# Joined h2 products in raw buffers, and GpSimd casts for the first feed-forward block

## The chip, the core and the metric

The kernel runs on one core of one Trainium2 chip. The metric is device time in microseconds of one execution. The core's engines are named in the profile as PE (TensorE, matrix products; PEld its weight loads), DVE (VectorE), ACT (ScalarE), POOL (GpSimd) and SP (SyncE, which issues the DMAs). Each engine works through its own list of instructions; between engines they wait for each other by semaphores.

## The reference

One decoder layer for 256 prompt tokens and 8 x 4 sample tokens (288 tokens in all). Cut to what the change touches:

```python
mod = (silu(c) @ w_ada + b_ada).reshape(n, N_MOD, 1, D_MODEL)
sh_m, sc_m, gt_m, sh_f, sc_f, gt_f = [mod[:, i] for i in range(N_MOD)]
...
x = x + gt_m * (merged @ w_out)
h2 = _rms(x, g_ffn) * (1 + sc_f) + sh_f
gate, up = jnp.split(h2 @ w_ffn_in, 2, axis=-1)
x = x + gt_f * ((silu(gate) * up) @ w_ffn_out)
...
y = _rms(x, g_final)
```

D_MODEL is 2048, D_FF 5632. `h2` is the second modulation; the "root" is the reciprocal root of the mean square of `x`, one factor for each token.

## The kernel before

Activations lie with features on the 128 partitions and the 288 tokens along a row: `x` is 16 tiles of 128 x 288. Weights stream from memory in blocks of 128 x 2048 (1 MB) into a ring of five raw buffers (`RAW = 5`). Products are made at nearly fp32 precision from two parts each: `hi` is the operand rounded to fp32r, `lo` is what the rounding left. A product of a weight tile with an activation tile is three matmuls: hi with hi, hi with lo, lo with hi.

A weight block is split in four segments of 512 columns. `Blk.high` (line 452) casts a segment to `hi` on ScalarE, `Blk.low` (line 464) subtracts on VectorE to get `lo`. There are four `hi` and four `lo` buffers (`SPB = 4`), so a segment can be cast only when TensorE has done its products with the segment four before it.

The stretch in question is the start of the feed-forward part:

- Four blocks `fk` (class `KBlk`) make the first four output tiles of the first feed-forward product from gained but not yet normalised tiles of `x` (`xg`), since the root of the new `x` is not known yet. Each has four segments, and each segment serves one tile of `xg` with 12 matmuls of 128 x 298.
- While they run, `rstd2` and `norm2` make the root and spread it over the partitions (`rb2`), and `mk_h2` makes the 16 tiles of `h2` in three portions: tiles 0 to 5 ahead of the second fk block in the program, 6 to 10 ahead of the third, 11 to 15 ahead of the fourth.
- Then the blocks `fi` follow, the rest of the first feed-forward product, each one output tile over all 16 tiles of `h2` (48 matmuls of 128 x 288). The first of them needs all 16 tiles of `h2` in turn.

A tile of `h2` passes through `modulate` (line 303): VectorE multiplies the tile of `x` with the root (`normed`, into a slot buffer); ScalarE applies gain and shift to the 256 prompt columns (`affine`) and GpSimd does so for the 32 sample columns in two operations (lines 311 and 312); ScalarE casts the result to `hi`; VectorE subtracts for `lo`. The tiles of this chain come from a pool `t` of five buffers.

Up to this stretch the order on ScalarE, VectorE and SyncE is pinned by hand; from the step after the wE blocks on (line 1062) a scheduler orders each engine's instructions by readiness and place in the program. Most instructions of VectorE, ScalarE and SyncE go through one helper and bear line 115 in the profile.

Of the kernel before, what the change touches and what calls it, by code (L numbers as in the profile page):

```python
# [7 lines left out]
F32 = mybir.dt.float32  # L8
F32R = mybir.dt.float32r
ALU = mybir.AluOpType  # L10
AF = mybir.ActivationFunctionType

P = 128
D = 2048
T = 288
# [7 lines left out]
RAW = 5  # L23
# [43 lines left out]
def decoder_kernel(tc, d):  # L67
    nc = tc.nc
    with ExitStack() as es:
        def pool(name, bufs=1, **kw):  # L70
            return es.enter_context(tc.tile_pool(name=name, bufs=bufs, **kw))

        pc = pool("const")
        pw = pool("wstream")
        pslot = pool("slots", SLOTS)
        ptmp = pool("tmp", 5)
        pps = pool("psum", 4, space=bass.MemoryType.PSUM)
        _body(tc, nc, d, pc, pw, pslot, ptmp, pps)


def _body(tc, nc, d, pc, pw, pslot, ptmp, pps):
    ids = [0]

    def nm(s):
        ids[0] += 1
        return f"{s}_{ids[0]}"

    def const(name, shape, dt=F32):
        return pc.tile(shape, dt, tag=name, name=name)

    def slot(dt=F32, shape=(P, T)):
        return pslot.tile(list(shape), dt, tag="s", name=nm("s"), padded_shape=[P, TU])

    def tmp(n=T):
        return ptmp.tile([P, n], F32, tag="t", name=nm("t"), padded_shape=[P, TU])
# [10 lines left out]
    class Pinned:  # L106
        def __init__(self, eng):
            self.eng, self.on, self.last = eng, True, None
# [13 lines left out]
    V, A, G, PE, SY = Pinned(nc.vector), Pinned(nc.scalar), nc.gpsimd, nc.tensor, Pinned(nc.sync)  # L122
# [16 lines left out]
    x = const("x", [P, 16, T])  # L139
# [27 lines left out]
    gm2 = const("gm2", [P, 16, NC])  # L167
# [58 lines left out]
    def sam(ap):  # L226
        return ap.rearrange("p (b s) -> p b s", s=NS)

    def bc4(ap):
        return ap.unsqueeze(2).to_broadcast([P, NB, NS])  # L230
# [10 lines left out]
    def upper(a, n=T):  # L241
        hi = slot(F32R, (P, n))
        A.copy(halves(hi, n), parity(a, n))
        return hi

    def lower(a, hi, n=T):
        lo = slot(F32R, (P, n))
        V.tensor_tensor(halves(lo, n), parity(a, n), halves(hi.bitcast(F32), n), ALU.subtract)
        return lo
# [5 lines left out]
    def normed(kt, rb):  # L255
        t = slot()
        V.tensor_tensor(t, x[:, kt, :], rb, ALU.mult)
        return t
# [10 lines left out]
    def warm(n, after=None):  # L269
        ps = psmisc()  # L270
        with behind(after):
            for _ in range(n):
                PE.matmul(ps[:, :P], ones, ones, start=True, stop=True)
# [9 lines left out]
    class Modulate:  # L283
# [13 lines left out]
        def high(self):  # L297
            self.hi = upper(self.h)
# [4 lines left out]
    def modulate(ks, get, gm, sh0, out):  # L303
        hs, his = {}, {}

        def affine(k, t):
            h = tmp()
            A.activation(
                h[:, :TP], t[:, :TP], AF.Identity, bias=mod[:, sh0 + k, 0:1], scale=gm[:, k, 0:1]
            )  # L310
            G.tensor_tensor(sam(h[:, TP:]), sam(t[:, TP:]), bc4(gm[:, k, 1:]), ALU.mult)  # L311
            S["aff"] = G.tensor_tensor(sam(h[:, TP:]), sam(h[:, TP:]), bc4(mod[:, sh0 + k, 1:]), ALU.add)
            hs[k], his[k] = h, upper(h)

        def finish_(k):
            out[k] = (his[k], lower(hs[k], his[k]))

        ts = {}
        n = len(ks)
        for i in range(n + 2):  # L320
            if i < n:
                ts[i] = get(ks[i])
            if 1 <= i <= n:
                affine(ks[i - 1], ts.pop(i - 1))
            if i >= 2:
                finish_(ks[i - 2])
# [16 lines left out]
    class Step:  # L343
        defer = False
        after, lead = None, 0
        raw = None
# [79 lines left out]
    class Blk(Step):  # L426
        def __init__(self, name, idx, rhs, sink, n=T):
            self.name, self.idx, self.rhs, self.sink, self.n = name, idx, rhs, sink, n
            self.k0, self.nk, self.nm = STREAMS[name]
            n = self.nk * self.nm  # L430
            self.per = -(-n // -(-n // SEG))
            self.segs = [(s, min(n, s + self.per)) for s in range(0, n, self.per)]
            self.his, self.parts, self.then = [], [], {}
            self.cuts = self.mate = self.wide = None
            self.apart = False

        def load(self, at=0, n=None):
# [12 lines left out]
            SY.dma_start(self.raw[:, a:b], d[self.name][self.idx][:, a:b])  # L450

        def high(self):
            s, e = self.segs[len(self.his)]
            hi = pw.tile([P, (e - s) * 128], F32R, tag="hi", name=nm("hi"), bufs=SPB, padded_shape=[P, SEG * 128])
            for a, b, raw in self.spans(s, e):
                self.cast = A.copy(hi[:, a:b], raw)
            self.his.append(hi)

        def spans(self, s, e):
# [90 lines left out]
    def ada(name):  # L550
        u = units[name]
        return [Ada(u, b) for b in range(16 // u[3])]


    S = {"strict": True}
# [274 lines left out]
    h2, xg = {}, {}  # L830
# [11 lines left out]

    def mk_h2(k0, k1):
        def f():
            modulate(range(k0, k1), lambda k: normed(k, S["rb2"]), gm2, 48, h2)

        return Do(f)

# [3 lines left out]
    def sink_fi(i, ps):  # L852
        f, up = i // 2, i % 2
        if not up:
            S["gate"] = ps
            return
        pg = S.pop("gate")
        t = tmp()
        A.activation(t, pg[:, :T], AF.Tanh, scale=0.5)
        V.scalar_tensor_tensor(t, t, 1.0, pg[:, :T], ALU.add, ALU.mult)  # L860
        V.scalar_tensor_tensor(t, t, 0.5, ps[:, :T], ALU.mult, ALU.mult)
        act[f] = split(t)
# [125 lines left out]
    def weave(main, side, a, b):  # L988
        out, n = [], len(side)
        done = 0  # L990
        for i, s in enumerate(main):
            out.append(s)
            want = n if i >= b else max(0, (i - a + 1) * n // (b - a + 1))
            for v in side[done:want]:
                out += v
            done = max(done, want)
        return out
# [54 lines left out]
    steps = [Do(silu), Do(lambda: warm(10)), *aA[:2], Do(lambda: warm(1, aA[1].last)), aA[2]]  # L1052
# [29 lines left out]
    def eight(blks):  # L1082
        for b in blks[1:5]:
            b.apart = True
        return blks
# [16 lines left out]
    def ffin(q):  # L1102
        fi = [Blk("fi", i - 4, h2.__getitem__, lambda j, ps: sink_fi(j + 4, ps)) for i in range(max(4, 22 * q), 22 * q + 22)]
        return fi
# [6 lines left out]
    fk[0].then = {(1, 1): [rstd2], (2, 2): [norm2]}  # L1111
    steps += [Do(fk[0].split), fk[0], Do(lambda: fk[1].split()), mk_h2(0, 6), fk[1], mk_h2(6, 11), fk[2], mk_h2(11, 16), fk[3]]
    a5 = ada("a5")
    steps += weave(ffin(0), [eight(a5[:8]), eight(a5[8:])], 0, 17)
    for q in range(3):
        nxt = ffin(q + 1)
        steps += nxt[:2] + ffout(q) + nxt[2:]
# [171 lines left out]
```

## Time and profile before

| | us |
|---|---|
| median of 3 runs | 1527.36 |
| lowest, highest | 1526.99, 1528.14 |
| the profiled execution | 1527.27 |
| its span (first to last instruction) | 1525.5 |

TensorE's clock was granted at 0.998 of full speed. In the views that follow, a row of the timeline has the start in us from the span's start, the duration, engine, line, operation, output and inputs with the numbers of the buffers left out, the shape, and how many instructions the row merges; in brackets the idle time of the engine before it and what ended it. A row of the groups has line, engine, operation, names and shapes, the count, then busy us and mean ns of one, then idle time before them and its releasers. The chain of waits follows the program's end back from one releaser to the next.

### The profile page before, as it was taken

What the parts mean: (1) busy time and instruction counts of PE and PEld (TensorE: products, weight loads), DVE (VectorE), ACT (ScalarE), POOL (GpSimd) and SP (SyncE); (2) the same over time, 40 slices, a digit from 0 to 9 for tenths busy, and PEclk for the clock granted to TensorE, in tenths of its full rate; (3) what the DMA queues carried; (4) which work ended last, traced back from release to release, by engine and by line L of the source; (5) the groups of instructions that cost most, each with busy time, mean ns of one, the idle gap of its engine ahead of it and who ended that gap; (6) DMA issues with size and microseconds to landing.
All of it is one profiled execution on the core that took longest, in us unless ns stands there. A gap on an engine that the chain in (4) does not pass through costs nothing.

```text
span 1525.5 us, 31733 instructions
## 1 busy us (share of the span) xinstructions
PE 1513.2 (99%) x12596; PEld 1447.8 (95%) x12596; DVE 987.8 (65%) x2000; ACT 743.7 (49%) x1381; POOL 124.1 (8%) x251
## 2 busy tenths in 40 slices
PE   9999999999999999999999999999999999999998
PEld 7898999999989998989999899999999999999997
DVE  5876567878856666757954466555665556655575
ACT  5543354644445444447844344444444444444465
POOL 2268010000100000002300000000000000000000
PEclk9999999999999999999999999999999999999999
DMA  9877875777877788865489656454565545655452
GB/s 370 336 291 279 358 275 184 287 267 268 309 281 291 290 277 310 268 250 190 165 305 337 230 172 222 176 183 143 173 221 178 182 150 167 217 186 173 144 180 92
DMA packets 74436, 357.70 MB, mean 234 GB/s; under 512 B 8384, under 2 KB 28640, under 8 KB 44080
## 3 DMA queue, kind: packets, MB, share of 16 engines
q1 hardware_dynamic: 73936, 354.95, 65.1%
q8 instruction: 98, 1.61, 0.4%
q0 software_dynamic: 352, 0.73, 0.1%
q14 instruction: 50, 0.41, 0.1%
HBM read 352.56 MB, written 3.09 MB: 233 GB/s over the span
## 4 chain that ended last, share of the span: by engine, by line
PE 92%; DMA 0%; DVE 0%; ACT 0%; issue 0%; DVEq 0%; POOL 0%; POOLq 0%
PE pm L493 28%; PE pm L495 28%; PE pm L494 28%; PE ada L383 4%; PE px L267 1%; DMA raw<-in_aE 0%; PE pm L527 0%; PE pm L528 0%; PE pm L529 0%; DVE lo L115 0%; PE pm L267 0%; PE px L529 0%; PE px L528 0%; PE px L527 0%; PE px L405 0%
## 5 line engine op out<-in xcount | busy, mean ns | idle before, releaser
L493 PE MATMUL pm<-s,hi 128*128 128x288 f32 (+1 forms) x3704 | 1063.7, 287 | 0.7 <-ACT s L115 0.5
L495 PE MATMUL pm<-s,lo 128*128 128x288 f32 (+1 forms) x3704 | 1059.9, 286 | 1.1 <-DVE lo L115 1.1
L494 PE MATMUL pm<-s,hi 128*128 128x288 f32 (+1 forms) x3704 | 1059.6, 286 | 0.0
L115 DVE TENSOR_TENSOR lo<-raw,hi 128x512 fp32r<-128x512 f32 (+1 forms) x966 | 662.0, 688 | 410.5 <-ACT hi L115 396.0
L115 ACT CAST hi<-raw 128x512 fp32r<-128x512 f32 (+1 forms) x966 | 584.2, 607 | 664.7 <-PE pm L494 591.8
L493 PEld LDWEIGHTS pm<-s,hi 128*128 128x128 f32 x3704 | 700.0, 189 | 13.4 <-issue 9.0
L495 PEld LDWEIGHTS pm<-s,lo 128*128 128x128 f32 x3704 | 700.0, 189 | 1.8 <-DVE lo L115 1.8
L494 PEld LDWEIGHTS pm<-s,hi 128*128 128x128 f32 x3704 | 700.1, 189 | 0.1
L383 PE MATMUL ada<-raw,cs 128*32 128x512 f32 (+3 forms) x768 | 75.8, 525 | 1.7 <-DMA raw<-in_aA 1.0
L115 DVE TENSOR_TENSOR s<-pm,s 128x288 f32<-128x288 f32 x128 | 57.6, 454 | 18.6 <-PE pm L495 18.4
L932 POOL TENSOR_TENSOR r<-r,mhalf 128x3 f32<-128x3 f32 x1 | 0.9, 862 | 768.4 <-DVE r L115 768.4
L115 ACT CAST s<-t 128x288 fp32r<-128x288 f32 (+1 forms) x109 | 50.8, 468 | 25.1 <-DVE t L115 21.6
L383 PEld LDWEIGHTS ada<-raw,cs 128*32 128x32 f32 x768 | 21.5, 109 | 37.5 <-issue 26.9
L115 DVE TENSOR_TENSOR s<-t,s 128x288 fp32r<-128x288 f32 (+1 forms) x109 | 51.0, 470 | 8.2 <-ACT s L115 8.1
L115 DVE SCALAR_TENSOR_TENSOR t<-t,pm 128x288 f32<-128x288 f32 x84 | 37.8, 450 | 11.1 <-PE pm L495 11.1
L115 DVE SCALAR_TENSOR_TENSOR x<-pm,mod,x 128x256 f32<-128x256 f32 (+1 forms) x81 | 38.1, 472 | 2.4 <-PE pm L495 2.4
L629 POOL TENSOR_TENSOR s<-s,rb 128x288 f32<-128x288 f32 x40 | 37.1, 928 | 0.0
L278 POOL TENSOR_TENSOR t<-x,gm 128x32 f32<-128x32 f32 x16 | 7.9, 492 | 250.3 <-DVE acc L115 237.9
L115 DVE SCALAR_TENSOR_TENSOR s<-pm,s 128x288 f32<-128x288 f32 x48 | 24.4, 509 | 0.0
L630 POOL TENSOR_TENSOR s<-s 128x32 f32<-128x32 f32 x48 | 23.9, 499 | 0.0
L311 POOL TENSOR_TENSOR t<-s,gm 128x32 f32<-128x32 f32 x28 | 12.3, 439 | 138.7 <-DVE gm L115 69.9
L115 ACT ACTIVATE t<-x 128x288 f32<-128x288 f32 (+2 forms) x32 | 13.7, 429 | 19.2 <-DVE x L115 19.2
(140 smaller groups left out, 543.9 us busy)
## 6 DMA issues: line engine op xcount, KB each, us to landing
raw<-in_fi SPq DMA_DIRECT2D x84, 1024.0 KB, 4.9
raw<-in_a SPq DMA_DIRECT2D x48, 1024.0 KB, 5.0
raw<-in_f SPq DMA_DIRECT2D x64, 704.0 KB, 4.1
raw<-in_wD SPq DMA_DIRECT2D x36, 1024.0 KB, 8.7
raw<-in_wC SPq DMA_DIRECT2D x20, 896.0 KB, 6.9
raw<-in_aE SPq DMA_DIRECT2D x16, 1024.0 KB, 7.5
s<-in_a SPq DMA_DIRECT2D x128, 128.0 KB, 5.6
raw<-in_wo SPq DMA_DIRECT2D x16, 1024.0 KB, 5.5
```

The source lines that it names most:

```text
L115: i = f(*args, **kw)
L267: return in_order(op(*args, **kw))
L278: G.tensor_tensor(sam(a[:, TP:T]), sam(x[:, k, TP:]), bc4(gm[:, k, 1:]), ALU.mult)
L311: G.tensor_tensor(sam(h[:, TP:]), sam(t[:, TP:]), bc4(gm[:, k, 1:]), ALU.mult)
L383: PE.matmul(acc[32 * j : 32 * j + 32, c], cs[:, kt, :], self.raw[2 * j + h] if self.apart else self.raw[:, o : o + w], start=(kt < ks), st ...
L493: PE.matmul(ps[:, : self.n], wh, ah, start=first, stop=False)
L494: PE.matmul(ps[:, : self.n], wh, al, start=False, stop=False)
L495: self.last = in_order(PE.matmul(ps[:, : self.n], wl, ah, start=False, stop=last))
L629: G.tensor_tensor(a[:, :T], a[:, :T], S[rb], ALU.mult)
L630: G.tensor_tensor(sam(a[:, TP:T]), sam(a[:, TP:T]), bc4(a[:, T + 1 : T + NC]), ALU.add)
L932: G.tensor_tensor(r, r, mhalf, ALU.pow)
```

## The change

Two edits. `mk_h2` no longer multiplies tile by tile: it takes one buffer of the raw ring for each portion and multiplies up to three neighbouring tiles of `x` with the root in one VectorE instruction (128 x 864, or 128 x 576 where two are left), the root repeated along the tiles. The chain behind it reads its tile out of that buffer. And the first fi block gets a `caster`: its four casts to `hi` are made by GpSimd's `tensor_copy` instead of ScalarE's copy.

```diff
-            self.cuts = self.mate = self.wide = None
+            self.cuts = self.mate = self.wide = self.caster = None
...
         def high(self):
+            copy = self.caster or A.copy
             s, e = self.segs[len(self.his)]
             hi = pw.tile([P, (e - s) * 128], F32R, tag="hi", name=nm("hi"), bufs=SPB, padded_shape=[P, SEG * 128])
             for a, b, raw in self.spans(s, e):
-                self.cast = A.copy(hi[:, a:b], raw)
+                self.cast = copy(hi[:, a:b], raw)
             self.his.append(hi)
...
     def mk_h2(k0, k1):
         def f():
-            modulate(range(k0, k1), lambda k: normed(k, S["rb2"]), gm2, 48, h2)
+            raw = pw.tile([P, 2048], F32, tag="raw", name=nm("raw"), bufs=RAW, padded_shape=[P, 2048])
+            ts = {}
+
+            def get(k):
+                if k not in ts:
+                    ks = range(k, min(k + 3, k1))
+                    t = raw[:, T * (k - k0) : T * (ks.stop - k0)].rearrange("p (k t) -> p k t", t=T)
+                    V.tensor_tensor(t, x[:, k : ks.stop, :], S["rb2"].unsqueeze(1).to_broadcast([P, len(ks), T]), ALU.mult)
+                    ts.update({j: t[:, j - k, :] for j in ks})
+                return ts.pop(k)
+
+            modulate(range(k0, k1), get, gm2, 48, h2)
...
-    steps += weave(ffin(0), [eight(a5[:8]), eight(a5[8:])], 0, 17)
+    fi0 = ffin(0)
+    fi0[0].caster = G.tensor_copy
+    steps += weave(fi0, [eight(a5[:8]), eight(a5[8:])], 0, 17)
```

The scheduler puts the instructions of three engines into another order. The names below: `raw_9329`, `raw_9421` and `raw_9513` are the weights of the second, third and fourth fk block, `raw_9605` those of the first fi block; `raw_9781`, `raw_9898` and `raw_10007` hold joined products; `hi` and `lo` are weight segments, `t` and `s` the tiles of `h2` on their way.

On VectorE, where the first portion of `h2` meets the third fk block, there stood before:

```order
L115 TENSOR_TENSOR s_9791<-x,rb_9748 128x288
L115 TENSOR_TENSOR s_9799<-t_9785,s_9789 128x288
L115 TENSOR_TENSOR lo_9779<-raw_9329,hi_9777 128x512
L115 TENSOR_TENSOR s_9801<-x,rb_9748 128x288
L115 TENSOR_TENSOR s_9809<-t_9793,s_9797 128x288
L115 TENSOR_TENSOR s_9811<-x,rb_9748 128x288
L115 TENSOR_TENSOR lo_9845<-raw_9421,hi_9843 128x512
L115 TENSOR_TENSOR s_9819<-t_9803,s_9807 128x288
L115 TENSOR_TENSOR s_9821<-x,rb_9748 128x288
L115 TENSOR_TENSOR s_9829<-t_9813,s_9817 128x288
L115 TENSOR_TENSOR lo_9849<-raw_9421,hi_9847 128x512
```

and now:

```order
L115 TENSOR_TENSOR lo_9779<-raw_9329,hi_9777 128x512
L115 TENSOR_TENSOR raw_9781<-x,rb_9748 128x864 x2
L115 TENSOR_TENSOR lo_9836<-raw_9421,hi_9834 128x512
L115 TENSOR_TENSOR s_9795<-t_9783,s_9787 128x288
L115 TENSOR_TENSOR s_9804<-t_9789,s_9793 128x288
L115 TENSOR_TENSOR s_9812<-t_9798,s_9802 128x288
L115 TENSOR_TENSOR s_9820<-t_9806,s_9810 128x288
L115 TENSOR_TENSOR s_9828<-t_9814,s_9818 128x288
L115 TENSOR_TENSOR s_9830<-t_9822,s_9826 128x288
L115 TENSOR_TENSOR lo_9840<-raw_9421,hi_9838 128x512
L115 TENSOR_TENSOR lo_9844<-raw_9421,hi_9842 128x512
L115 TENSOR_TENSOR lo_9848<-raw_9421,hi_9846 128x512
```

The joined products stand behind the last difference of the second fk block, whose raw buffer they take, and all six tiles of the portion stand between the first and the second weight segment of the third fk block (`lo_9836`, `lo_9840`; before `lo_9845`, `lo_9849`).

On ScalarE at the same place there stood before:

```order
L115 CAST hi_9843<-raw_9421 128x512
L115 CAST s_9807<-t_9803 128x288
L115 ACTIVATE t_9813<-s_9801,mod,gm_91 128x256
L115 ACTIVATE t_9823<-s_9811,mod,gm_91 128x256
L115 CAST s_9817<-t_9813 128x288
L115 CAST hi_9847<-raw_9421 128x512
L115 CAST s_9827<-t_9823 128x288
```

and now:

```order
L115 CAST hi_9834<-raw_9421 128x512
L115 ACTIVATE t_9783<-raw_9781,mod,gm_91 128x256
L115 ACTIVATE t_9789<-raw_9781,mod,gm_91 128x256
L115 CAST s_9787<-t_9783 128x288
...
L115 ACTIVATE t_9814<-raw_9781,mod,gm_91 128x256
L115 ACTIVATE t_9822<-raw_9781,mod,gm_91 128x256
L115 CAST s_9818<-t_9814 128x288
L115 CAST s_9826<-t_9822 128x288
L115 CAST hi_9838<-raw_9421 128x512
```

Twelve instructions of `h2` stand between the first and the second cast of the third fk block, where four did.

On GpSimd, at the end of its work on `h2`, there stands now:

```order
L311 TENSOR_TENSOR t_9931<-raw_9898,gm_91 128x32
L312 TENSOR_TENSOR t_9931<-t_9931,mod 128x32
L457 CAST hi_10052<-raw_9605 128x512
L457 CAST hi_10056<-raw_9605 128x512
L457 CAST hi_10060<-raw_9605 128x512
L311 TENSOR_TENSOR t_10009<-raw_10007,gm_91 128x32
L311 TENSOR_TENSOR t_10015<-raw_10007,gm_91 128x32
L312 TENSOR_TENSOR t_10009<-t_10009,mod 128x32
L312 TENSOR_TENSOR t_10015<-t_10015,mod 128x32
L457 CAST hi_10064<-raw_9605 128x512
L311 TENSOR_TENSOR t_10024<-raw_10007,gm_91 128x32
L312 TENSOR_TENSOR t_10024<-t_10024,mod 128x32
```

Before, the operations of lines 311 and 312 followed each other without a cast among them. Three of the new casts stand ahead of the last portion's five tiles, and one between its second and its third. TensorE's order stays but for two matmuls with `lo` of the fk blocks: the first of the third block's second segment goes behind the next two, and the first of the fourth block's third segment behind the next one.

## The prediction

> **What bounds the kernel now.** I read the page first, then the chain of waits, then the timeline of each engine between 719 and 762 us, the only stretch whose order changes.
>
> ```profile
> span 1525.5 us, 31733 instructions
> PE 1513.2 (99%) x12596; PEld 1447.8 (95%) x12596; DVE 987.8 (65%) x2000; ACT 743.7 (49%) x1381; POOL 124.1 (8%) x251
> PE 92%; DMA 0%; DVE 0%; ACT 0%; issue 0%; DVEq 0%; POOL 0%; POOLq 0%
> ```
>
> TensorE is the bound: whatever makes it wait is added to the span, and nothing later gives it back. So the question is how long TensorE waits near the change, now and after. The timeline of PE:
>
> ```profile
> 726.54 0.29 PE L529 MATMUL pm<-s,lo 128*128 128x298 f32 x1
> ...
> 732.75 0.29 PE L527 MATMUL px<-s,hi 128*128 128x298 f32 x1
> ...
> 734.27 0.29 PE L527 MATMUL px<-s,hi 128*128 128x298 f32 x1
> ...
> 741.87 0.29 PE L527 MATMUL px<-s,hi 128*128 128x298 f32 x1
> ...
> 744.98 0.29 PE L493 MATMUL pm<-s,hi 128*128 128x288 f32 x1
> ...
> 748.04 0.39 PE L493 MATMUL pm<-s,hi 128*128 128x288 f32 x1
> 748.27 0.29 PE L494 MATMUL pm<-s,hi 128*128 128x288 f32 x1
> 748.77 0.39 PE L495 MATMUL pm<-s,lo 128*128 128x288 f32 x1 [0.21 <-DVE lo L115]
> 748.99 0.29 PE L493 MATMUL pm<-s,hi 128*128 128x288 f32 x1
> ...
> 751.57 0.29 PE L493 MATMUL pm<-s,hi 128*128 128x288 f32 x1
> ```
>
> The rows are the last product of fk block 1, the first of fk block 3, its second segment, the third segment of fk block 4, the first fi block, and the second (751.57). A segment (12 products) takes 734.27 - 732.75 = 1.52 us, 0.127 a product. The fi block's 48 products take 6.59 us; at (751.57 - 748.99) / 21 = 0.123 each they would take 5.88. So TensorE loses **0.71 us** here. The chain of waits names why:
>
> ```profile
> 743.65 0.58 POOL t L312
> 744.33 0.30 issue
> 744.63 0.64 ACT hi L115
> ...
> 747.37 0.62 ACT hi L115
> 748.02 0.70 DVE lo L115
> 748.77 0.39 PE pm L495
> ```
>
> The block's third weight segment is cast late because ScalarE and VectorE are full of h2 work. A relief of ScalarE can win those 0.71 us and no more.
>
> **The change part by part.** Durations in this stretch, on ScalarE (timeline) and on VectorE and GpSimd (groups, mean ns of one):
>
> ```profile
> 738.75 1.09 ACT L115 ACTIVATE t<-s,mod,gm 128x256 f32<-128x256 f32 x2
> 739.75 0.82 ACT L115 CAST s<-t 128x288 fp32r<-128x288 f32 x2
> 740.48 1.13 ACT L115 CAST hi<-raw 128x512 fp32r<-128x512 f32 x2
> 741.52 0.60 ACT L115 ACTIVATE t<-s,mod,gm 128x256 f32<-128x256 f32 x1
> ```
>
> ```profile
> L115 DVE TENSOR_TENSOR lo<-raw,hi 128x512 fp32r<-128x512 f32 x19 | 13.3, 707 | 1.2 <-ACT hi L115 1.2
> L115 DVE TENSOR_TENSOR s<-t,s 128x288 fp32r<-128x288 f32 x16 | 7.5, 473 | 0.6 <-ACT s L115 0.6
> L115 DVE TENSOR_TENSOR s<-x,rb 128x288 f32<-128x288 f32 x16 | 7.4, 479 | 1.0 <-ACT rb L115 1.0
> L311 POOL TENSOR_TENSOR t<-s,gm 128x32 f32<-128x32 f32 x16 | 7.0, 440 | 8.7 <-DVE s L115 8.5
> L312 POOL TENSOR_TENSOR t<-t,mod 128x32 f32<-128x32 f32 x16 | 6.3, 396 | 1.3
> ```
>
> By the starts, back to back: an affine 0.50 us, a tile cast 0.365, a weight cast 0.52 (0.61 until its result is there). On VectorE a weight difference takes 0.70, a tile difference 0.47. On GpSimd a tile takes 0.44 + 0.40 and some 0.1 of gaps, 0.93.
>
> *The joined products.* Sixteen become six. The row for two tiles in one instruction stands at the end of the program, its factor in PSUM:
>
> ```profile
> L115 DVE TENSOR_TENSOR x<-x,px 128x576 f32<-128x576 f32 x2 | 1.5, 752 | 0.9 <-PE px L267 0.9
> ```
>
> From 479 to 752 ns is 0.27 for a tile, so three cost 1.03 us. VectorE wins 16 x 0.48 - 4 x 1.03 - 2 x 0.75 = 2.1 us, off the path. What costs is the new order. The product needs a raw buffer, so it comes after the last difference of fk block 2, where before the first products preceded it; and on ScalarE all six tiles stand ahead of the second weight segment of fk block 3 (the rows above).
>
> *First stall.* Fk block 1's last product ends at 726.8; the weight cast that waits for its buffer ends at 727.4, its difference at 728.1, the first product of three at 729.1. ScalarE then does two affines (730.1), waits for GpSimd's third operation (0.44 + 0.44 + 0.40 and gaps: 730.5), casts two (731.3), two affines (732.3). The fourth tile on GpSimd ends at 732.85, the sixth at 734.7; the casts follow at 733.2 and 735.1. Only now the weight cast: 735.7, against 734.27 when TensorE wants it: 1.45 late. The difference is there at 736.4, 0.15 behind TensorE, which the new order lets do four products first (735.75 + 4 x 0.127 = 736.25): **1.6 us**. Queued behind these casts are the block's other two segments and the first of fk block 4, all earlier than their use.
>
> *Second stall.* On VectorE the second join (three tiles, two) waits for the differences 736.4 + 3 x 0.6 = 738.2; its first product ends at 739.2. Five tiles stand ahead of the third weight segment of fk block 4: affines 740.2, GpSimd's third operation 740.65, casts 741.4, affines 742.4, casts 743.3 (GpSimd's fourth tile 742.95), affine 743.8, weight cast 744.4, difference 745.1. TensorE, 1.6 later, wants it at 743.47: 0.95, and 0.3 more for the difference (due after three products, 744.83): **1.25 us**. It reaches the fi block at 744.98 + 2.85 = 747.83.
>
> *The four weight casts on GpSimd.* No row has a 128x512 cast there. The nearest, in mean ns:
>
> ```profile
> L562 POOL TENSOR_TENSOR s<-x 128x288 f32<-128x288 f32 x8 | 6.4, 833 | 6.5 <-DMA x<-in_x 6.5
> L757 POOL TENSOR_TENSOR s<-s,cp 128x256 f32<-128x256 f32 x4 | 4.3, 1106 | 3.2 <-DMA s<-in_wsg 3.2
> L280 POOL MEMSET t<- 128x1 f32 x16 | 1.6, 97 | 0.0
> L739 POOL MEMSET s<- 128x256 f32 x4 | 1.2, 312 | 78.1 <-DVE t L115 42.6 <-PE px L267 35.5
> L294 POOL TENSOR_TENSOR t<-s,gm 128x32 f32<-128x32 f32 x4 | 0.9, 242 | 14.7 <-DVE gm L115 10.9 <-DVE s L115 3.9
> ```
>
> From below a write without a read: 97 + 2 x 215 = 0.53 us. From above two operands: 2 x 1106 = 2.2. One operand lies between: (833 - 242) / 256 = 2.3 ns a column for two, half of it gives 0.24 + 480 x 1.15 = 0.8; beside a busy VectorE I take **1.0**. The Trainium skill (GPSIMD Engine Reference, side-by-side cycle accounting) gives 769 ns for 512 elements in a tight loop; by it the sum would be some 0.2 us smaller. No run here shows it yet.
>
> *Third stall.* Two casts run from 743.95 to 745.95, covered by fk block 4. The third waits for TensorE to release the buffer (746.2): 747.2. Behind it in GpSimd's queue stand the last five tiles; their product comes at 747.85 (after the differences at 746.2 and 746.8). GpSimd does two tiles (749.55), the fourth cast (750.55), three tiles (753.35). ScalarE's cast of the last tile, with a weight cast of the next block ahead of it, ends at 754.2, the difference at 754.95. TensorE, from 747.83, wants it at 747.83 + 46 x 0.123 = 753.45: **1.5** of waiting, against 0.71 before, so +0.8.
>
> *Fourth.* The next fi block needs a PSUM bank that two VectorE operations (0.45 each, behind that last difference) must read: 755.75, while TensorE is ready at 755.25: **+0.5**.
>
> *Hidden.* The joins take three raw buffers, so later loads wait for them; a load lands in 4.9 us:
>
> ```profile
> raw<-in_fi SPq DMA_DIRECT2D x84, 1024.0 KB, 4.9
> ...
> 798.77 7.02 PE ada L383 x96
> ```
>
> The third fi block's load waits for the first join's last reader (735.1) and lands at 740.0; TensorE wants it two blocks after 747.83, at 759.6. The fourth waits for the second join (743.9): 748.8 against 765.5. Behind them in SyncE's queue stand the slices of a5, first used at 798.77. So nothing; without that lead each load would cost up to 4.9 us.
>
> Sum: 1.6 + 1.25 + 0.8 + 0.5 = 4.15 us. The profiled execution took 1527.27 (span 1525.5 and 1.8 around it), 0.1 under the median of 1527.36: **1531.4 us**.
>
> **Bounds.** With GpSimd's operations at the free 242 ns and its cast at 0.53, the first stall falls to 0.8, the second to 0.65, and the 0.71 is won: +0.75, 1528.0. With the cast at 2.2 GpSimd ends at 757.2, the last difference at 758.8, 5.35 late: 1.6 + 1.25 + 4.65 + 0.5 = +8.0, 1535.3.
>
> **The rivals.**
> *Hidden after all.* The lower bound: not slower beyond what can be told. For it: GpSimd waits much of this stretch (8.7 us behind L311 above), so its mean of 440 ns may hold contention that a changed order avoids. Against: 729.1 + 6 x 0.865 on ScalarE alone is already 734.3, when TensorE wants the cast's result. It decides if GpSimd's tile is under 0.7. 1528.0.
> *Dear casts.* The two-operand price, 1535.3; only L757 speaks for it.
> *A locked port.* VectorE's differences against GpSimd:
>
> ```profile
> L115 DVE TENSOR_TENSOR lo<-raw,hi 128x512 fp32r<-128x512 f32 x25 | 21.9, 880 | 10.3 <-ACT hi L115 10.2
> ...
> L629 POOL TENSOR_TENSOR s<-s,rb 128x288 f32<-128x288 f32 x34 | 32.1, 945 | 0.0
> ...
> L115 DVE TENSOR_TENSOR lo<-raw,hi 128x512 fp32r<-128x512 f32 x125 | 86.4, 691 | 67.0 <-ACT hi L115 66.1
> ```
>
> At 95 to 140 us GpSimd never rests and a difference takes 880 ns, at 1000 to 1200 GpSimd is idle and it takes 691. If one held the other off for a whole instruction, GpSimd would wait out the second product of each join (1.03, 0.75, 0.75) before its first tile: 4.15 + 2.5 = +6.6, 1533.9. Against: 0.19 us of loss is far from the 0.8 or more of a whole instruction. The Trainium skill (SBUF — State Buffer, two separate sides) states just such an exclusive lock for the whole instruction; the 880 agrees that the two collide, not that one fully blocks.
> *Faster.* Sixteen short products gone and 2.1 us taken off ScalarE: the casts no longer queue there and the 0.71 us disappear, the fk blocks unhurt. 1526.6. Against: the order on ScalarE above.
>
> **How the numbers follow.** Forecast (+2.5 to +6) 0.58; dear casts 0.10; locked port 0.09; hidden 0.17; the 0.71 won 0.04; something outside these that helps 0.02. A measurement can tell about 0.2%, 3.05 us. Of the forecast 0.05 lies under that. Same: 0.05 + 0.17 + 0.04 = 0.26; slower 0.53 + 0.19 = 0.72; faster 0.02. The range goes from 1528.2, inside the hidden case, to 1536.5, above the dear casts, since both could add.
>
> **What would show it.** TensorE waiting at the second segment of fk block 3 (about 1.6 us, for a ScalarE cast), at the third of fk block 4, at the end of the first fi block; a first product at 1.0 us on VectorE; GpSimd casts near 1.0. The forecast is wrong if no wait of 1 us stands before a segment of fk block 3, or if a GpSimd cast takes 2 us or more.

## The result, and the profile after

The changed kernel takes 1532.53 us (median of 7 runs, 1531.99 to 1533.74), the kernel before on the same chip 1527.05: a ratio of 1.0033, 95% interval 1.0023 to 1.0043. It is slower by 5.5 us in the medians; in the profiled executions the span grew from 1525.5 to 1530.3 us, by 4.8. The ratio is that of the means (1532.58 and 1527.50 us), so it is not the quotient of the medians. The first rows of the page after:

```profile
span 1530.3 us, 31718 instructions
PE 1514.4 (99%) x12596; PEld 1447.6 (95%) x12596; DVE 987.5 (65%) x1990; ACT 742.2 (49%) x1377; POOL 125.7 (8%) x255
```

TensorE has the same work. The 4.8 us are new idle time, and the timeline of PE shows where:

```profile
734.13 0.29 PE L530 MATMUL pm<-s,lo 128*128 128x298 f32 x1
735.90 0.39 PE L528 MATMUL px<-s,hi 128*128 128x298 f32 x1 [1.48 <-ACT hi L115]
...
736.38 0.29 PE L529 MATMUL pm<-s,hi 128*128 128x298 f32 x1
736.62 0.39 PE L530 MATMUL px<-s,lo 128*128 128x298 f32 x1
...
743.70 0.29 PE L530 MATMUL pm<-s,lo 128*128 128x298 f32 x1
744.61 0.39 PE L528 MATMUL px<-s,hi 128*128 128x298 f32 x1 [0.63 <-ACT hi L115]
...
754.20 0.29 PE L496 MATMUL pm<-s,lo 128*128 128x288 f32 x1
754.77 0.39 PE L494 MATMUL pm<-s,hi 128*128 128x288 f32 x1 [0.29 <-ACT s L115]
755.51 0.39 PE L495 MATMUL pm<-s,hi 128*128 128x288 f32 x1 [0.35 <-DVE s L115]
755.74 0.29 PE L496 MATMUL pm<-s,lo 128*128 128x288 f32 x1
756.33 0.36 PE L494 MATMUL pm<-s,hi 128*128 128x288 f32 x1 [0.31 <-DVE s L115]
```

A wait is read here as the time from one product's start to the next, less the usual 0.127 us (fk) or 0.123 us (fi). By that TensorE waits 1.97 us at the second segment of fk block 3 (735.90 - 734.13 and the short gaps behind it), 1.24 at the third segment of fk block 4 (from 743.70), 1.89 in the last part of the first fi block, and 0.55 at the second, which waits for a bank of PSUM (the memory that this kernel's matmuls write to; the tiles lie in the other one, SBUF): 5.65 in all. Before it was 0.78 (the 0.71 and some 0.07). The difference is 4.87, the whole change of the span within 0.1. These four places are the ones that the prediction names. The waits of PE name the engines: ScalarE's weight casts for the first two, and its and VectorE's work on the last tiles of h2 behind them.

```profile
PE px L528 <- ACT hi L115: 2.1, 2, 1.5
PE pm L495 <- DVE s L115: 0.4, 1, 0.4
```

The joined products and the tile work behind them, in the groups of VectorE and GpSimd (720 to 757 us):

```profile
L115 DVE TENSOR_TENSOR raw<-x,rb 128x576 f32<-128x576 f32 x2 | 1.5, 748 | 0.0
...
L311 POOL TENSOR_TENSOR t<-raw,gm 128x32 f32<-128x32 f32 x16 | 7.7, 485 | 12.1 <-DVE raw L115 12.1
L312 POOL TENSOR_TENSOR t<-t,mod 128x32 f32<-128x32 f32 x16 | 4.9, 313 | 0.8
```

A join of two takes 0.75 us as forecast. One of three takes 1.05 (below) three times out of four; the one of the last portion takes 1.46. The new weight casts on GpSimd, by duration:

```profile
L457 POOL CAST hi<-raw x4: 607/627/823, 743.0 to 750.5; 128x512 fp32r<-128x512 f32 x4
```

That is minimum, median and maximum in ns: shorter than the 1.0 us taken for them. But the operations of line 311 grew from a mean of 440 ns to 485, and the first ones of each portion are the long ones. The timelines of VectorE and GpSimd where the first portion starts:

```profile
728.11 2.03 DVE L115 TENSOR_TENSOR raw<-x,rb 128x864 f32<-128x864 f32 x2
730.05 0.73 DVE L115 TENSOR_TENSOR lo<-raw,hi 128x512 fp32r<-128x512 f32 x1
```

```profile
729.31 1.58 POOL L311 TENSOR_TENSOR t<-raw,gm 128x32 f32<-128x32 f32 x2 [5.51 <-DVE raw L115]
730.85 0.44 POOL L312 TENSOR_TENSOR t<-t,mod 128x32 f32<-128x32 f32 x2
731.25 0.24 POOL L311 TENSOR_TENSOR t<-raw,gm 128x32 f32<-128x32 f32 x1
```

Free, this operation takes 0.24 us. The two in the first row last 925 and 686 ns: the first runs until 0.1 us behind the second join (728.11 + 2.03 = 730.14), the second until 0.1 us behind the weight difference (730.78). Both of those VectorE instructions read two operands in SBUF.

### The profile page after: what moved, and what is told of

Read it like the earlier page. It is cut to its first block, busy times and chain, and to the rows that moved or that the text cites. A ratio compares the mean times of both kernels' runs of the same rounds, so it can differ in the third digit from the quotient of the medians.

```text
span 1530.3 us, 31718 instructions
## 1 busy us (share of the span) xinstructions
PE 1514.4 (99%) x12596; PEld 1447.6 (95%) x12596; DVE 987.5 (65%) x1990; ACT 742.2 (49%) x1377; POOL 125.7 (8%) x255
## 4 chain that ended last, share of the span: by engine, by line
PE 50%; DVE 0%; POOL 0%; ACT 0%; issue 0%; DVEq 0%; ACTq 0%
PE pm L494 16%; PE pm L495 16%; PE pm L496 16%; PE ada L383 1%; PE px L267 0%; POOL t L311 0%; ACT t L115 0%; PE pm L267 0%; DVE raw L115 0%; DVE lo L115 0%; POOL t L312 0%; DVE s L115 0%; DVEq L1285 0%; ACT hi L115 0%; ACT s L115 0%
## 5 line engine op out<-in xcount | busy, mean ns | idle before, releaser
L115 DVE TENSOR_TENSOR acc<-acc,t 128x288 f32<-128x288 f32 x36 | 16.4, 456 | 8.7 <-ACT t L115 8.7
```

The lines of the kernel that those rows point to most:

```text
L115: i = f(*args, **kw)
```

## The experiments

Twelve kernels ran, each beside the kernel before on the same chip. In one table: the median, the ratio to before, and TensorE's waits in the profiled execution, read as above, in us.

| kernel | median | ratio, 95% interval | fk 3 | fk 4 | fi 1 | fi 2 | sum |
|---|---|---|---|---|---|---|---|
| before | 1527.05 | 1 | 0 | 0.07 | 0.71 | 0 | 0.78 |
| changed | 1532.53 | 1.0033 (1.0023-1.0043) | 1.97 | 1.24 | 1.89 | 0.55 | 5.65 |
| e1 joins alone | 1532.41 | 1.0034 (1.0021-1.0047) | 1.95 | 1.21 | 1.90 | 0.95 | 6.0 |
| e2 GpSimd casts alone | 1529.22 | 1.0014 (1.0004-1.0024) | 0 | 0.06 | 1.81 | 1.07 | 2.9 |
| e3 joins outside the ring | 1531.86 | 1.0031 (1.0021-1.0042) | 0.09 | 1.40 | 1.82 | 0.70 | 4.0 |
| e5 segments woven in | 1532.1 | 1.0033 (1.0021-1.0044) | 0.88 | 1.79 | 1.71 | 0.55 | 4.9 |
| e7 last portion unjoined | 1531.2 | 1.0028 (1.0017-1.0039) | 1.97 | 1.25 | 1.00 | 0.51 | 4.7 |
| e8 root from PSUM, first portion | 1530.56 | 1.0021 (1.0012-1.0030) | 1.08 | 0.44 | 2.15 | 0.55 | 4.2 |
| e11 root from PSUM, all portions | 1529.87 | 1.0017 (1.0008-1.0026) | 1.07 | 0.03 | 1.45 | 0.55 | 3.1 |
| e6 two GpSimd casts alone | 1528.25 | 1.0005 (0.9996-1.0014) | 0 | 0.07 | 1.29 | 0.13 | 1.5 |
| e9 before, four segments woven | 1527.51 | 1.0002 (0.9993-1.0011) | 0 | 0.06 | 0 | 0.73 | 0.8 |
| e10 before, three woven late | 1526.85 | 0.9999 (0.9990-1.0008) | 0 | 0.10 | 0 | 0.28 | 0.4 |
| e12 before, root from PSUM | 1526.78 | 0.9998 (0.9989-1.0007) | 0 | 0 | 0 | 0.14 | 0.1 |
| e13 e12 with three woven late | 1526.55 | 0.9995 (0.9986-1.0004) | 0 | 0 | 0 | 0.36 | 0.4 |

The kernel before, run beside them, had medians of 1527.26 us (e1 to e5), 1527.58 (e7 to e10) and 1527.28 (e6 and e11 to e13); each ratio is to its own. The profiled executions of some kernels reach this stretch up to 1.8 us later than before's, mostly since TensorE waited longer for loads in the first 200 us; so waits are compared here, and medians, not spans.

### One edit at a time

`e1_products` is the changed kernel without the caster:

```diff
     fi0 = ffin(0)
-    fi0[0].caster = G.tensor_copy
```

> Joined products alone; ScalarE casts all weights as before. Theory A (the joins and the order that comes of them are the whole loss): TensorE waits 2.0 us at the second segment of fk block 3 and 1.2 us at the third of fk block 4 as in the changed kernel, and 1.5 to 2.5 us in the first fi block, since the last portion of h2 starts as late as there; 4.5 to 5.5 us over the kernel before, near 1532. Theory B (the third wait comes from weight casts standing in GpSimd's queue): the first two waits stay, the fi block waits no more than before (0.7 us); 3.0 to 3.5 us over, near 1530.3.

`e2_caster` is the kernel before with the caster:

```diff
+    fi0 = ffin(0)
+    fi0[0].caster = G.tensor_copy
```

> GpSimd's four casts alone; tile by tile products as before. Theory A: no wait at fk blocks 3 and 4, a cast takes 0.6 to 0.8 us, the fi block waits 0.5 to 1.0 us (0.7 before) because the last two casts stand behind the last tile's operations on GpSimd; within 0.5 us of the kernel before. Theory B: the fi block waits 1.5 us or more, at least 1 us over the kernel before.

The joins alone give the whole loss (6.0 us of waits, 1532.41), as theory A had it. The first fi block waits as long without the GpSimd casts (1.90 us), but elsewhere: mostly for ScalarE's cast of its fourth weight segment, where the changed kernel waits for the last tiles of h2. The caster alone should have cost next to nothing and cost 2.9 - 0.8 = 2.1 us of waits: theory A was missed there, and B held. GpSimd and ScalarE of `e2_caster`, then VectorE:

```profile
744.71 0.45 POOL L311 TENSOR_TENSOR t<-s,gm 128x32 f32<-128x32 f32 x1
745.24 0.34 POOL L312 TENSOR_TENSOR t<-t,mod 128x32 f32<-128x32 f32 x1
745.53 0.83 POOL L457 CAST hi<-raw 128x512 fp32r<-128x512 f32 x1
746.33 0.45 POOL L311 TENSOR_TENSOR t<-s,gm 128x32 f32<-128x32 f32 x1
746.86 0.34 POOL L312 TENSOR_TENSOR t<-t,mod 128x32 f32<-128x32 f32 x1
...
748.22 1.16 POOL L457 CAST hi<-raw 128x512 fp32r<-128x512 f32 x2
```

```profile
745.61 0.47 ACT L115 CAST s<-t 128x288 fp32r<-128x288 f32 x1 [0.37 <-POOL t L312]
745.99 0.60 ACT L115 ACTIVATE t<-s,mod,gm 128x256 f32<-128x256 f32 x1
747.23 0.46 ACT L115 CAST s<-t 128x288 fp32r<-128x288 f32 x1 [0.64 <-POOL t L312]
```

```profile
742.72 1.28 DVE L115 TENSOR_TENSOR s<-x,rb 128x288 f32<-128x288 f32 x2
...
748.86 1.06 DVE L115 TENSOR_TENSOR lo<-raw,hi 128x512 fp32r<-128x512 f32 x1 [0.69 <-POOL hi L457]
```

A cast of 0.83 us stands between the tiles in GpSimd's queue, and ScalarE waits for the tile behind it: from 738 us on it waits 1.7 us for line 312, against 0.2 before, and 1.0 of that is the two waits shown. The casts wait for the tiles too: the third and fourth start at 748.22, behind the last tile's operations, and VectorE waits 0.69 us for the third before it can make the difference that TensorE waits for. VectorE's row at 742.72 shows that GpSimd can hold off VectorE: while a GpSimd cast runs (742.85, 0.83 us), two tile products take 1.28 us. The same two in the kernel before:

```profile
742.61 0.86 DVE L115 TENSOR_TENSOR s<-x,rb 128x288 f32<-128x288 f32 x2
```

The two edits do not add up: 5.2 us of waits for the joins, 2.1 for the casts, 4.9 for both. With the joins h2 is late already, and the GpSimd casts make it no worse; whether they give some of it back the medians do not tell (1532.53 with them, 1532.41 without).

`e6_two_casts` is `e2_caster` with only the first two casts on GpSimd:

```diff
-            copy = self.caster or A.copy
+            copy = self.caster if self.caster and len(self.his) < 2 else A.copy
```

> The kernel before, with only the first two of the four weight casts of the first fi block on GpSimd. Theory Q (the caster alone costs because its casts stand among the tiles in GpSimd's queue): the waits behind the last two casts (0.7 us at the block's last third, 1.0 us in the second fi block) go, the 1.1 us at the second segment stays or shrinks, time 1527.8 to 1528.5. Rival: the casts themselves are too slow, each later than ScalarE's would be; the time stays at 1529.2.

The waits of the second fi block fall from 1.07 to 0.13, the one at the second segment stays at 1.09; 1528.25, inside the range expected for the queue. The cast of that segment stands behind four tile operations on GpSimd (lines 311 and 312, as in the rows above) and its difference behind two on VectorE, however few casts there are.

### Ring buffer and order on ScalarE

`e3_own_buffer` has both edits, with the joins in a buffer of their own (one, reused) in place of the raw ring:

```diff
-            raw = pw.tile([P, 2048], F32, tag="raw", name=nm("raw"), bufs=RAW, padded_shape=[P, 2048])
...
-                    t = raw[:, T * (k - k0) : T * (ks.stop - k0)].rearrange("p (k t) -> p k t", t=T)
+                    t = ptmp.tile([P, len(ks) * T], F32, tag="ev", name=nm("ev"), bufs=1, padded_shape=[P, 3 * T])
+                    t = t.rearrange("p (k t) -> p k t", t=T)
```

> Both edits, but the joined products lie in a buffer of their own (three tiles, shared with the buffer that takes the ada sums, which is free then) and not in the raw ring, so the first join need not wait for fk block 2's last weight difference. Two small buffers elsewhere are merged to make room. Theory C (the wait for the ring's buffer makes the h2 work late): first join near 725.4 instead of 728.1 us, no wait of 0.5 us at the fk blocks, 0.5 to 1.2 us in the fi block, within 0.7 us of the kernel before. Rival D (a joined product costs by itself, since a long VectorE operation holds GpSimd off): waits of about 1 us remain at the fk blocks and the kernel is 2 us or more over.

VectorE of `e3_own_buffer`:

```profile
725.36 1.06 DVE L115 TENSOR_TENSOR ev<-x,rb 128x864 f32<-128x864 f32 x1 [1.02 <-ACT rb L115]
...
729.11 1.06 DVE L115 TENSOR_TENSOR ev<-x,rb 128x864 f32<-128x864 f32 x1 [0.41 <-POOL t L312]
...
733.44 1.06 DVE L115 TENSOR_TENSOR ev<-x,rb 128x864 f32<-128x864 f32 x1 [0.77 <-ACT t L115]
```

The first join starts 2.75 us earlier, and the wait at fk block 3 is gone. ScalarE's order changed with the buffer: the second weight segment of that block stands behind three tiles, not six. So this run alone does not tell the earlier start from the order; `e5_woven`, below, has three tiles there too, with the ring's late start, and still waits 0.88 us. But each further join now waits for the readers of the one buffer, and fk block 4 and the first fi block wait about as long as in the changed kernel (1.40 and 1.82 us). Theory C had the start and the first wait right; the time falls little, as rival D had it.

`e5_woven` has both edits, and writes the next block's weight segments between the tiles of a portion, not behind them:

```diff
+            nxt = next(b for b in blks if not b.his or len(b.his) < len(b.segs))
...
             def get(k):
+                if k > k0 and (k - k0) % 2 == 0 and nxt.raw is not None and len(nxt.his) < len(nxt.segs):
+                    nxt.high()
+                    nxt.low()
                 if k not in ts:
```

> Both edits with the products in the raw ring as in the changed kernel, but in the program each weight segment of the next block is written between two tiles of a portion, so that on ScalarE the second segment of fk block 3 stands behind three tiles and not six. Theory E (the lump of tiles ahead of the weight cast is what stalls): the waits at fk block 3 fall from 2.0 to 0.5 us or less and the one at fk block 4 goes; the fi block still waits 1.5 to 2.5 us, since its portion still waits for the ring; 1.5 to 2.5 us over the kernel before. If the late start alone counts (theory C without E): the first wait stays above 1.5 us.

The stall moves: 0.88 us at fk block 3, now at its third segment, and 1.79 at fk block 4, now at the fourth. Neither theory held. One weight cast of 0.6 us set ahead makes the tiles, and the casts behind them, that much later. So the order settles which product waits more than how much TensorE waits: the sum falls from 5.65 to 4.9.

`e7_two_portions` has both edits but multiplies tiles 11 to 15 one by one, without a raw buffer:

```diff
-            modulate(range(k0, k1), get, gm2, 48, h2)
+            modulate(range(k0, k1), get if k0 < 11 else lambda k: normed(k, S["rb2"]), gm2, 48, h2)
```

> Both edits, but the last portion of h2 (tiles 11 to 15) is multiplied tile by tile, so it takes no raw buffer; GpSimd still casts the first fi block. Theory R (the wait in the first fi block comes from the third join, which waits for the raw buffer of fk block 4 until 746.8 us): the products of that portion start 1.5 to 2 us earlier, TensorE's waits at fk blocks 3 and 4 stay at 2.0 and 1.2 us, the one in the first fi block falls from 1.9 to 0.8 us or less, and the time is about 1531.0. Rival Q (GpSimd's queue, with the weight casts among the tiles, makes that wait, as it did with the caster alone): the first two fi blocks together still wait 2.0 us or more, and the time is 1532 or more.

The first two waits are unchanged, the one in the first fi block falls from 1.89 to 1.00, between the two theories, and the time to 1531.2. The 1.00 stands elsewhere, at the difference of the block's third weight segment. VectorE of `e7_two_portions`:

```profile
746.03 0.68 DVE L115 TENSOR_TENSOR lo<-raw,hi 128x512 fp32r<-128x512 f32 x1
746.63 0.81 DVE L115 TENSOR_TENSOR s<-x,rb 128x288 f32<-128x288 f32 x2
```

Without the join of this portion about half of the third stall is gone. But the join's wait for the raw buffer is not the reason: unjoined and without that buffer the first product still starts at 746.63 (the third join at 746.79, in an execution that is 0.4 us ahead here), behind the weight differences that VectorE's order puts first. What is won is that one product is there after some 0.45 us, where the first join of this portion takes 1.46 (its row stands further below).

### Who holds off whom

`e8_psum_root` has both edits, and the joins of the first portion read the root from the PSUM bank in which it is made:

```diff
         A.copy(S["rb2"], ps)
+        S["bps"] = ps
...
-S["rb2"].unsqueeze(1).to_broadcast([P, len(ks), T])
+(S["rb2"] if k0 else S["bps"]).unsqueeze(1).to_broadcast([P, len(ks), T])
```

Of the changed line only the operand is shown.

> Both edits, but the joined products of the first portion read the root from the PSUM bank in which it was made and not from its copy in SBUF, so that these two VectorE instructions have one operand in SBUF instead of two. Theory L (GpSimd's short operations wait out a VectorE instruction that reads two operands in SBUF): the first operation of line 311 beside the second join takes 0.45 us or less instead of 0.93, and TensorE's wait at fk block 3 falls from 2.0 to between 1.5 and 1.8 us; the time is about 1532.0. Rival N (the long duration has nothing to do with VectorE's operands): it stays at 0.6 us or more, the wait at 2.0, the time at 1532.4.

VectorE and GpSimd at the place shown above for the changed kernel:

```profile
728.55 2.02 DVE L115 TENSOR_TENSOR raw<-x,px 128x864 f32<-128x864 f32 x2
730.49 0.69 DVE L115 TENSOR_TENSOR lo<-raw,hi 128x512 fp32r<-128x512 f32 x1
```

```profile
729.75 0.44 POOL L311 TENSOR_TENSOR t<-raw,gm 128x32 f32<-128x32 f32 x2 [5.51 <-DVE raw L115]
730.15 0.45 POOL L312 TENSOR_TENSOR t<-t,mod 128x32 f32<-128x32 f32 x2
730.55 0.72 POOL L311 TENSOR_TENSOR t<-raw,gm 128x32 f32<-128x32 f32 x1
...
739.04 0.62 POOL L311 TENSOR_TENSOR t<-raw,gm 128x32 f32<-128x32 f32 x1 [5.22 <-DVE raw L115]
```

The joins take the same 1.0 us each and stand at the same place; only one operand is in another memory. Now four GpSimd operations run at their free 0.24 us beside the second join. The next (730.55) meets the weight difference, whose operands are both in SBUF, and is held to 0.72 again; so is the first beside the second portion's joins, which still read the copy (0.62). The wait at fk block 3 falls from 1.97 to 1.08 us, more than expected; both held operations became short. From fk block 4 on the scheduler's order differs as well, so only that first wait is a clean reading.

`e11_psum_all` extends this to all portions, and leaves the order on TensorE, ScalarE and GpSimd as in `e8_psum_root`:

```diff
-(S["rb2"] if k0 else S["bps"]).unsqueeze(1).to_broadcast([P, len(ks), T])
+S["bps"].unsqueeze(1).to_broadcast([P, len(ks), T])
```

> Both edits, and the joined products of all three portions read the root from its PSUM bank, not from its copy in SBUF. Theory L (GpSimd waits out VectorE instructions with two SBUF operands): GpSimd's operations beside the joins take 0.45 us or less in all portions, TensorE's wait at fk block 3 stays at the 1.1 us of the run with the first portion alone, the one at fk block 4 is 0.5 us or less, those in the first fi block fall below 2.0 us together, and the time is 1530.2 or less. Rival O (what is left is the order on ScalarE and the ring wait of the third join): nothing changes against that run, 1530.6.

```profile
738.85 0.24 POOL L311 TENSOR_TENSOR t<-raw,gm 128x32 f32<-128x32 f32 x1 [5.22 <-DVE raw L115]
739.17 0.24 POOL L312 TENSOR_TENSOR t<-t,mod 128x32 f32<-128x32 f32 x1
739.37 0.70 POOL L311 TENSOR_TENSOR t<-raw,gm 128x32 f32<-128x32 f32 x1
```

GpSimd's row at 739.04 (0.62) has become 0.24, and the expectation of theory L held. Fk block 4 waits 0.03 us, the two fi blocks 2.0 together against 2.7 in `e8_psum_root`, and the waits sum to 3.1 us against 5.65 in the changed kernel. Of the 2.55 us between, 0.9 (fk block 3 in `e8_psum_root`) and 1.1 (from there to `e11_psum_all`, where only one pair of VectorE's instructions changed places) are what the joins with two operands in SBUF cost through GpSimd; the other 0.5 may be the order that came with `e8_psum_root`.

### Can the 0.71 us be had

`e9_woven_before` and `e10_woven_late` are the kernel before with weight segments of the first fi block written ahead of the last tiles of h2 (four, one ahead of each of tiles 12 to 15; three, ahead of tile 15). The second:

```diff
-            modulate(range(k0, k1), lambda k: normed(k, S["rb2"]), gm2, 48, h2)
+            nxt = next(b for b in blks if len(b.his) < len(b.segs))
+
+            def get(k):
+                for _ in range(3) if k == 15 else ():
+                    nxt.high()
+                    nxt.low()
+                return normed(k, S["rb2"])
+
+            modulate(range(k0, k1), get, gm2, 48, h2)
```

> The kernel before (products tile by tile, casts on ScalarE), with the four weight segments of the first fi block written between the tiles of the last portion of h2, so that the third segment's cast comes ahead of the last two tiles on ScalarE and not behind them. Theory A (the 0.71 us of before is this cast's place in ScalarE's order): the wait in the first fi block is 0.2 us or less and the time 1526.5, 0.7 under before. Rival: the last tile of h2 is now late instead and TensorE waits 0.5 us or more for it at the end of the block; the time is 1527.3 or more.

> The kernel before, with three of the four weight segments of the first fi block written ahead of the last tile of h2 only, so that just the third cast moves, ahead of one affine and one cast of a tile. Theory A: the wait in the first fi block is 0.2 us or less, the last tile is in time, the time is 1526.5. Rival: the cast then still comes late (after 747.2 us) or the last tile does, 0.4 us or more of wait stay, the time is 1527.0 or more.

In both the wait in the first fi block is gone. In the first it comes back as 0.73 us at the second fi block, whose first weight difference stands behind the reading of fk's PSUM banks on VectorE, as it did before. Counted from the first product of the first fi block it starts 0.3 us later than before (6.01 against 5.71), behind a later last tile, and TensorE comes to it 0.7 us sooner. So the rival had the size right and the place wrong. In the second 0.28 come back.

`e12_psum_before` is the kernel before with the products reading the root from PSUM, and `e13_psum_woven` is that together with the weaving of `e10_woven_late`. The edit to both:

```diff
         A.copy(S["rb2"], ps)
+        S["bps"] = ps
...
-normed(k, S["rb2"])
+normed(k, S["bps"])
```

> The kernel before with one change: the tile-by-tile products of h2 read the root from its PSUM bank. Theory L: GpSimd's operations of lines 311 and 312 fall from a mean of 440 and 396 ns to 350 or less; ScalarE's casts that waited for them come earlier, and the 0.71 us in the first fi block falls to 0.4 or less; the time is 1527.2 or less. Rival O (that wait is the place of the cast in ScalarE's order, behind the last tiles): 0.6 us or more stay, and the time is that of before.

> The kernel before, products reading the root from PSUM, and three weight segments of the first fi block written ahead of the last tile of h2. If both theories hold, TensorE waits 0.2 us or less anywhere in the stretch, and the time is 1526.5, some 0.8 under before, the least this stretch can give; if the first weight difference of the second fi block stays late, 0.3 us are left and the time is 1526.9.

GpSimd's groups of `e12_psum_before` in this stretch:

```profile
L312 POOL TENSOR_TENSOR t<-t,mod 128x32 f32<-128x32 f32 x16 | 6.0, 376 | 1.3
L311 POOL TENSOR_TENSOR t<-s,gm 128x32 f32<-128x32 f32 x16 | 5.7, 353 | 9.8 <-DVE s L115 9.0 <-ACT t L115 0.4
```

Line 311 falls from 440 to 353 ns, line 312 only from 396 to 376, both above the 350 expected. TensorE's waits fall to 0.14 us; the order on VectorE and ScalarE changed too, so this run does not tell which of the two did it. The weaving adds nothing to it: 0.36 us come back at the second fi block. The medians of e10, e12 and e13 lie 0.5 to 0.7 us under those of before beside them, about what the waits say, but every interval holds 1: no version is shown to beat the kernel before.

## Why the prediction held

**The bound, the places and the sign** held. TensorE waited at the four places named, for the engines named, and the waits account for the whole difference: 4.87 us against 4.15 forecast, 1532.5 against 1531.4.

**First stall**: 1.97 against 1.6. The first join was to start behind the difference at 728.1 and did (728.11). GpSimd's third operation was to end at 730.5; it ended at 731.1 (730.85 and one operation of 0.24), because the first two were held off by VectorE. Behind it the tiles ran faster than the 0.93 us taken for each on GpSimd (all six within 4.6 us from 729.31), so most of this was made good, and the weight cast came 0.2 us late. The remaining 0.2 is in three short gaps behind it, one of them for the difference.

**Second stall**: 1.24 against 1.25. That close a match is luck in part: the weight cast came some 0.15 us later than forecast, but TensorE, held longer at the first stall, 0.35 us later. **Fourth**: 0.55 against 0.5. **Hidden loads**: as forecast, TensorE waited for no load between 744 and 800 us.

**Third stall**: 1.89 against 1.5. Here sizes were off in opposite directions. The GpSimd casts take 0.61 to 0.82 us, not 1.0. But the first join took 1.46 us, not 1.03: it started while GpSimd's third cast ran. In `e1_products`, which has no cast there, the same join took 1.05. VectorE and GpSimd of the changed kernel, then VectorE of `e1_products`:

```profile
746.79 1.46 DVE L115 TENSOR_TENSOR raw<-x,rb 128x864 f32<-128x864 f32 x1
...
748.84 1.37 DVE L115 TENSOR_TENSOR lo<-raw,hi 128x512 fp32r<-128x512 f32 x2
```

```profile
746.69 0.65 POOL L457 CAST hi<-raw 128x512 fp32r<-128x512 f32 x1 [1.95 <-PE pm L529]
748.33 1.33 POOL L311 TENSOR_TENSOR t<-raw,gm 128x32 f32<-128x32 f32 x2 [0.99 <-DVE raw L115]
749.63 0.88 POOL L312 TENSOR_TENSOR t<-t,mod 128x32 f32<-128x32 f32 x2
```

```profile
746.86 1.05 DVE L115 TENSOR_TENSOR raw<-x,rb 128x864 f32<-128x864 f32 x1
```

And the first four tile operations behind it took 1.33 + 0.88 = 2.2 us against 1.7 from the means, held off by the second join and the weight differences. In the end the last tile's difference was done 0.5 us later than forecast, at 755.46, and TensorE had come 0.3 us later. That the size came near is luck in part: the forecast made this stall out of the GpSimd casts in the queue, and `e1_products`, without them, waits 1.90 us in the same block, for ScalarE.

**The locked port** was a rival with a chance of 0.09, and its mechanism is real. The argument against it, that long differences on VectorE lost only 0.19 us beside a busy GpSimd, was the wrong test: it asked for a mean of what VectorE loses, and the loss here is mostly that of GpSimd's short operations. One of 0.24 us that finds a VectorE instruction with two operands in SBUF running waits for its end. The Trainium skill (SBUF — State Buffer, two separate sides) says this of VectorE instructions with two inputs in SBUF against GpSimd operations that read SBUF; the traces agree (925 and 686 ns against 243 with one input in PSUM). One operation of `e1_products` even waited out three in a row, the second join and two weight differences (747.83 to 749.79):

```profile
748.06 1.83 POOL L311 TENSOR_TENSOR t<-raw,gm 128x32 f32<-128x32 f32 x1 [4.91 <-DVE raw L115]
```

What was wrong was the rival's price: 2.5 us on top of the sum, when the means of 440 and 396 ns already held such waits. Freed of the joins' share (`e11_psum_all`), the waits come to 3.1 us, 2.3 above before: the forecast of 4.15 lay between that and the 4.87 measured.

**The hidden case** fell. Its bound of 0.75 us was for GpSimd at 242 ns throughout, which no run has; with GpSimd free beside the joins alone (means of 414 and 329 ns) 2.3 us are left. **Dear casts** fell with 0.61 to 0.82 us. **Faster** fell: taking four casts off ScalarE alone cost 2.1 us, since the casts and the tile operations, which ScalarE waits for, then wait for each other in GpSimd's queue. The forecast priced the two edits as one chain and did not see that the caster alone is a loss; beside the joins that does not show.

**Not settled**: how the third stall divides between the order, the ring and the held-off operations. Each experiment moved it, and none removed it.

## What to carry to other kernels

Count instructions saved only on the engine that sets the end. Here the joins took VectorE 6.0 us where sixteen products took 7.4, time that nobody waited for, and made the first of three tiles ready later, which everybody waited for. And before small work is moved to an idle engine, look at what already waits for that engine's queue: a cast of 0.6 to 0.8 us between short operations is paid by whoever waits for the next of them, and the cast itself waits for those ahead of it.

## What the hardware showed that was not expected

The memory of one operand decided whether the joins on VectorE and GpSimd's operations disturbed each other. With the root in SBUF a GpSimd operation beside a join of the changed kernel took 627 to 925 ns, with the root in PSUM 0.24 us, while the join took 1.05 us either way. It works in the other direction too: beside a GpSimd cast two VectorE products took 1.28 us instead of 0.86, and a join 1.46 instead of 1.05. In `e11_psum_all` the same join also started beside a GpSimd cast, with the root in PSUM, and took 1.04. And a 128x512 cast to fp32r on GpSimd took 607 ns at best, about what ScalarE's takes until its result is there (0.61).
